# First layer's shift and scale by quarters of the features, with the first products behind each quarter

## Chip, cores and metric

The kernel runs on one core of a Trainium2 chip. The metric is the device time of one execution in microseconds (us). Three runs of the kernel before gave a median of 1486.53 us (1484.78 to 1489.08).

## What is computed

Two layers of a block over 1024 tokens x and 256 context tokens ctx with 1024 features, all in float32:

```
shift, scale, gate = split(silu(c) @ w_mod[l] + b_mod[l], 3)     # the same from c_ctx for ctx
h  = rms_norm(x, g_pre[l]) * (1 + scale) + shift                 # hc for ctx
y  = token_mixers(h @ w_in[l], hc @ w_in[l], ...)                # retention, spatial gating, short conv, gated delta
x  = x + gate * rms_norm(y @ w_out[l], g_post[l])                # ctx too, in layer 0
```

w_mod[l] has 1024 x 3072 elements, w_in[l] 1024 x 3856. So all of shift and scale (8.4 MB of w_mod) stands ahead of the first complete h of layer 0, and h ahead of every product with w_in. Feature j of h needs only columns j of shift and scale.

## The kernel before, in words

Tokens (x, then ctx) are cut into 10 tiles of 128 and into blocks of 512, 512 and 256; features are cut into 8 chunks of 128 (`KC`). h lies with features on partitions, as a high part h·h and a low part h·l (h minus its rounded high part); a weight is split in the same way into `whi` (ScalarE, line 479) and `wlo` (GpSimd, line 480). Each product is made of three matmuls: high by high, high by low, low by high. There are two kinds: token-major (`proj_tm`, PSUM tile `pt`, 272 columns with the gates' 16, lines 574 to 576; 24 matmuls a token tile) and feature-major (`projs`, PSUM tile `pj`, lines 540 to 542; 24 matmuls a block).

`first_h` is the first stage. It loads x of tiles 0 to 3, squares and sums each row (line 389), scales it (line 393), and turns it on TensorE (line 398). `mod(0)` loads w_mod in 16 loads of 128 rows by 1024 columns (line 266), first all of the shift, then all of the scale; each step makes four matmuls (line 268) that sum over the feature chunks, so shift and scale are known only when the last load has been used. `end` copies the sums, turns them and adds bias and g_pre (lines 278 to 289). Then `block` makes h for a block: block 0 (lines 434, 435, 439) from x turned beforehand, blocks 1 and 2 after a turn (lines 437 to 439); every third chunk's low part is made by GpSimd. `block(b)` also asks for x of the next block; it is called when `proj_tm` reaches tiles 0, 4 and 8.

The first product is `spatial_v` (token-major, with the gates); after it `gates`, then the key projection of the gated delta mixer (`delta_pair(l, 1)`, columns from 12 x 256, two strips of 128 columns over three blocks), and later the other mixers, drawn as filler beside the delta stages (`fillers`, `beside`).

All loads are issued from SyncE's one queue. `inorder` keeps the loads of the first stage in the order in which they are written down; otherwise the framework's planner orders each engine's instructions from dependencies and durations that it assumes, and lays the buffers in memory. A buffer's number of copies is its pool's: G 10, F 7, `q` 8, `raw` 2, `whi` and `wlo` 4; the next use of a copy waits until the one before is done.

`retention_pair` works block by block: scores `rsc` on TensorE (line 853), the scores times a constant mask on VectorE (line 857, mask kept in `base`), q times decay into `rqd` (line 863), then products into `ro` (lines 874, 881). `make_h` makes h of layer 1 beside the output products of layer 0 (lines 443 to 471).

Of the kernel before, what the change touches and what calls it, by code (L numbers as in the profile page):

```python
# [12 lines left out]
ALU = mybir.AluOpType  # L13
# [17 lines left out]
START = 5  # L31
KEPT = 2400
# [62 lines left out]
class Block:  # L95


    def __init__(self, ctx, tc, a, dbg=None):
        self.tc, self.nc, self.a, self.dbg = tc, tc.nc, a, dbg
        pool = lambda n, b, **k: ctx.enter_context(tc.tile_pool(name=n, bufs=b, **k))  # L100
        self.hp = pool("hp", 1)
        self.wp = pool("wp", 2)
        self.gp = pool("gp", 10)
        self.fp = pool("fp", 7)
        self.mp = pool("mp", 2)
        self.pj = pool("pj", 2, space=PSUM)
        self.pg = pool("pg", 2, space=PSUM)
        self.pf = pool("pf", 2, space=PSUM)
        self.pc = pool("pc", 1, space=PSUM)
        self.dp = pool("dp", 1, space=DRAM)  # L110
        self.uid = 0
        self.flow = iter(())
        self.lead = 0.0
        self.later = []
        self.loaded = None
        self.Hs = None
        self.both = {}
        self.rot = None
        self.layer = 0
# [56 lines left out]
    def setup(self):  # L176
# [4 lines left out]
                     ((C_ID, C_MASK), (C_MASK, C_TRI))}  # L181
# [75 lines left out]
    def mod(self, l):  # L257

        nc, a = self.nc, self.a
        pm = []  # L260

        def one(kc, half):
            if not pm:
                pm.append(self.pc.tile([P, 1024], F32, tag="cc", name="mod0"))
            w = self.slot("wm")[:, :D]
            self.inorder(nc.sync.dma_start(w, a["w_mod"][l, kc * P:(kc + 1) * P, half * D:(half + 1) * D]))
            for g in range(4):
                self.modded = nc.tensor.matmul(pm[0][32 * g:32 * g + 32, 256 * half:256 * half + 256], lhsT=self.s2[:, kc, :],
                                               rhs=w[:, 256 * g:256 * g + 256], start=(kc == 0), stop=(kc == KC - 1))

        def rows(half):
            if not pm:
                pm.append(self.psf("mod"))
            return pm[0][:, 256 * half:256 * half + 256]

        def end(half):
            ms = self.small([P, 256], "ms", 1)
            nc.scalar.copy(ms, pm[0][:, 256 * half:256 * half + 256])
            pt = self.psf("modT")
            for j in range(2):  # L280
                nc.tensor.transpose(pt[:, 128 * j:128 * j + 128], ms[:, 128 * j:128 * j + 128], self.ident)
            v = pt[:, :256].rearrange("p (j g q) -> p g j q", j=2, q=32)
            bm = self.fv[:, self.FV[("bmod", l)]].rearrange("p (s g j) -> p s g j", s=2, g=4)[:, half]
            gp = self.fv[:, self.FV[("gpre", l)]].rearrange("p (g j) -> p g j", g=4)
            for r in range(2):
                x = self.AB[l][:, r, 1 - half].rearrange("p (g j) -> p g j", g=4)
                nc.vector.tensor_tensor(x, v[:, :, :, r], bm, ALU.add)
                if half:
                    nc.vector.scalar_tensor_tensor(x, x, 1.0, gp, ALU.add, ALU.mult)

        steps = []
        for half in range(2):
            if l:
                steps += self.mod_rows(l, half, lambda half=half: rows(half))
            else:
                steps += [lambda kc=kc, half=half: one(kc, half) for kc in range(KC)]
            steps.append(lambda half=half: end(half))
        return steps

    def mod_rows(self, l, part, out):  # L300
# [11 lines left out]
        def step(j):  # L312
# [3 lines left out]
            with self.tc.manual_schedule(engines={PE}):  # L316
                for kc in (2 * j, 2 * j + 1):
                    for g in range(4):
                        nc.tensor.matmul(ps[32 * g:32 * g + 32], lhsT=self.s2[:, kc, :], rhs=w[kc, g // 2][:, 256 * (g % 2):256 * (g % 2) + 256],
                                         start=(kc == 0), stop=(kc == KC - 1))  # L320

        return [lambda: load(0)] + [lambda j=j: step(j) for j in range(KC // 2)]

    def quarter(self, nm):
        self.uid += 1
        return self.mp.tile([P, 512], F32, tag=f"q{self.layer}", name=f"{nm}{self.uid}", bufs=8)
# [49 lines left out]
    def first_h(self):  # L376
# [23 lines left out]

        self.new_h(0)
# [3 lines left out]
        for i, step in enumerate(self.mod(0)):  # L405
            if i == KC:
                turn_rows()
            step()
            if i < KC:
                for x in loads[i::KC]:  # L410
                    x()
            if START <= i < START + KC:
                kc = i - START
                if kc % 2 == 0:
                    xT.append(self.slot("xT", "G")[:, :1024].rearrange("p (j n) -> p j n", j=2))
                nc.scalar.copy(xT[-1][:, kc % 2], turn(kc, 0, 512, self.modded))

        def block(b, t0, n):
            if b < 2:
                t1 = t0 + n  # L420
                load(range(t1 // P, (t1 + BLOCKS[True][b + 1][1]) // P))
# [5 lines left out]
            A, B = self.AB[0][:, t0 // TL, 0], self.AB[0][:, t0 // TL, 1]  # L427
            for kc in range(KC):
                if kc % 2 == 0:
                    hb = xT[kc // 2] if b == 0 else self.slot("hb")[:, :2 * n].rearrange("p (j n) -> p j n", j=2)  # L430
                hf = hb[:, kc % 2]
                hi, lo = (self.h(s, kc, t0, n) for s in range(2))
                if b == 0:
                    nc.scalar.activation(hi, hf, AF.Identity, bias=B[:, kc:kc + 1], scale=A[:, kc:kc + 1])
                    nc.vector.tensor_scalar(hf, hf, A[:, kc:kc + 1], B[:, kc:kc + 1], ALU.mult, ALU.add)
                else:
                    nc.scalar.activation(hf, turn(kc, t0, n), AF.Identity, bias=B[:, kc:kc + 1], scale=A[:, kc:kc + 1])
                    nc.vector.tensor_copy(hi, hf)
                (nc.gpsimd if kc % 3 == 2 else nc.vector).tensor_tensor(lo, hf, hi.bitcast(F32), ALU.subtract)

        self.ahead = [lambda b=b, t0=t0, n=n: block(b, t0, n) for b, (t0, n) in enumerate(BLOCKS[True])]

    def make_h(self, l, t, x, held):
# [10 lines left out]
        xn = self.small([P, D], "xn", 1)  # L454
        nc.vector.tensor_scalar(xn, x, rs, None, ALU.mult)
        A, B = self.AB[l][:, r, 0], self.AB[l][:, r, 1]
        for q in range(2):
            pt = self.psf("xT")
            for j in range(4):
                kc = 4 * q + j  # L460
                self.after(nc.tensor.transpose(pt[:, j * P:(j + 1) * P], xn[:, kc * P:(kc + 1) * P], self.ident), held)
            hf = xn[:, 512 * q:512 * q + 512]
# [67 lines left out]
    def projs(self, l, blocks, *pairs):  # L530
# [3 lines left out]
        for t0, n in blocks:  # L534
            if self.ahead:
                self.ahead.pop(0)()
            for (hi, lo), (_, evac) in zip(W, pairs):
                b = self.bank("pj")
                for kc in range(KC):
                    nc.tensor.matmul(b[:, :n], lhsT=hi[kc], rhs=self.h(0, kc, t0, n), start=(kc == 0), stop=False)  # L540
                    nc.tensor.matmul(b[:, :n], lhsT=hi[kc], rhs=self.h(1, kc, t0, n), start=False, stop=False)  # L541
                    self.recent = nc.tensor.matmul(b[:, :n], lhsT=lo[kc], rhs=self.h(0, kc, t0, n), start=False, stop=(kc == KC - 1))  # L542
                    if kc % 2 and kc < KC - 1:
                        yield 6 * n / 2400
# [5 lines left out]

    def proj_tm(self, l, c0, tiles, evac, gates=False):

        nc = self.nc
        c1 = 15 * 256
        n = 272 if gates else 256
        w = []
        for j in range(4):
            hi, lo = (self.wtile(t, 2, n) for t in ("whi", "wlo"))
            raw = self.raw([P, 2, n])
            k = slice(2 * j, 2 * j + 2)  # L560
            self.inorder(nc.sync.dma_start(raw[:, :, :256], self.wcols(l, c0, 256)[:, k]))
            if gates:
                self.inorder(nc.sync.dma_start(raw[:, :, 256:], self.wcols(l, c1, 16)[:, k]))
            self.halve(hi, lo, raw)
            w.append((hi, lo))
        for t in range(NT if gates else len(tiles)):
# [3 lines left out]
            b = self.bank("pt")[:, cols]  # L570
            for kc in range(KC):
                hi, lo = (x[:, kc % 2, cols] for x in w[kc // 2])
                ah, al = (self.h(s, kc, t * P, P) for s in range(2))
                nc.tensor.matmul(b, lhsT=ah, rhs=hi, start=(kc == 0), stop=False)  # L574
                nc.tensor.matmul(b, lhsT=ah, rhs=lo, start=False, stop=False)  # L575
                nc.tensor.matmul(b, lhsT=al, rhs=hi, start=False, stop=(kc == KC - 1))  # L576
                if kc == 3:
                    yield 1.28
# [199 lines left out]
    def retention_pair(self, l, ctx, rp):  # L778
# [65 lines left out]
        mask = cst(C_MASK + rp * 256, 256).rearrange("p (h i) -> p h i", h=2)  # L844
        for t0, m in blocks:
            tiles = range(t0 // P, (t0 + m) // P)
            sc = []
            pSs = [self.psf("rsc") for _ in range(2)]
            with self.tc.manual_schedule(engines={PE}):
# [10 lines left out]
            qd = self.slot("rqd")[:, :2 * m].rearrange("p (d i) -> p d i", d=2)  # L860
# [720 lines left out]
    def run(self, out, layers=2):  # L1581
        self.setup()
        self.first_h()
        for l in range(layers):
# [3 lines left out]
            self.cols, self.made = self.columns(l), {}  # L1588
# [46 lines left out]
```

## Time and profile before

| | |
|---|---|
| median of 3 runs | 1486.53 us |
| profiled execution | 1490.67 us, its span 1488.9 us |
| mean granted TensorE clock | 0.957 |
| TensorE (PE) busy | 1383.5 us, 93% of the span |
| VectorE (DVE) busy | 733.0 us, 49% |
| ScalarE (ACT) busy | 452.7 us, 30% |
| GpSimd (POOL) busy | 332.6 us, 22% |
| chain that ended last, by engine | PE 73%, DVE 9%, issue 6%, DMA 4%, ACT 3%, POOL 3% |

Times are us from the start of the span. PE is TensorE's matmuls and PEld its weight loads; SPq are the loads that SyncE issues. A row of the timeline gives start, duration, engine, line, operation, output and inputs, and in brackets how long the engine was idle before it and what ended that. The granted clock is a share of 2.4 GHz; 0.50 is 1.2 GHz. A DMA share is the mean busy share of the 16 DMA engines in a stretch.

### The profile page before, as it was taken

To read this page: it belongs to the slowest core of one execution; us is meant where nothing else is said; L and a number is where in the kernel's file an instruction comes from. 1 tells how busy PE (TensorE), PEld (TensorE's weight loads), DVE (VectorE), ACT (ScalarE), POOL (GpSimd) and SP (SyncE) were. 2 spreads that over 40 slices of the span, in tenths; PEclk is the share of its full clock that TensorE was granted. 3 is DMA by queue.
4 is the path that set the end of the run, shared out by engine and by line. 5 is a ranking of instruction groups with operands and counts; after the bars stand their busy time and mean duration, and the time that the engine had idled before them with its cause. 6 is when DMAs were issued, how large, how long until landed. Compare 5 with 4: busy or idle time off the path is not lost.

```text
span 1488.9 us, 36109 instructions
## 1 busy us (share of the span) xinstructions
PE 1383.5 (93%) x15800; PEld 1154.1 (78%) x15800; DVE 733.0 (49%) x1357; ACT 452.7 (30%) x930; POOL 332.6 (22%) x265
## 2 busy tenths in 40 slices
PE   5789899889999999999999997997899999999997
PEld 2588788756787877788999985886667867878997
DVE  1657587244334746133444366395453476633132
ACT  3636422211201222332455536312121112233221
POOL 0233321112201311132122135112232112123220
PEclk9799979899999999999999998998899999999999
DMA  8415564126432212184234243635143103225451
GB/s 269 158 36 136 110 160 114 60 69 218 137 104 65 88 43 79 29 259 139 91 125 134 75 86 95 141 101 126 53 136 101 36 16 124 76 79 186 139 178 57
DMA packets 228392, 164.93 MB, mean 111 GB/s; under 512 B 112038, under 2 KB 195978, under 8 KB 228234
## 3 DMA queue, kind: packets, MB, share of 16 engines
q1 hardware_dynamic: 228234, 162.62, 37.5%
q8 instruction: 124, 2.03, 0.5%
q14 instruction: 34, 0.28, 0.1%
HBM read 122.34 MB, written 40.24 MB: 109 GB/s over the span
## 4 chain that ended last, share of the span: by engine, by line
PE 73%; DVE 9%; issue 6%; DMA 4%; ACT 3%; POOL 3%; SPq 0%; DVEq 0%; POOLq 0%; ACTq 0%
PE pj L540 13%; PE pj L541 12%; PE pj L542 12%; PE po L1526 4%; PE po L1528 4%; PE po L1527 4%; PE pt L574 3%; PE pt L576 2%; PE pt L575 2%; DMA wm<-in_w_mod 2%; PE gu L1316 1%; POOL wlo L480 1%; DVE lt L1158 1%; PE ro L874 1%; PE iq L1190 1%
## 5 line engine op out<-in xcount | busy, mean ns | idle before, releaser
L480 POOL TENSOR_TENSOR wlo<-raw,whi 128x512 fp32r<-128x512 f32 (+3 forms) x160 | 223.1, 1409 | 872.3 <-ACT whi L479 750.2
L540 PE MATMUL pj<-h0h,whi 128*128 128x512 f32 (+1 forms) x544 | 214.6, 394 | 11.3 <-ACT whi L479 10.6
L542 PE MATMUL pj<-h0h,wlo 128*128 128x512 f32 (+1 forms) x544 | 208.1, 382 | 4.7 <-POOL wlo L480 4.7
L540 PE MATMUL pj<-h1h,whi 128*128 128x512 f32 (+1 forms) x544 | 208.6, 383 | 0.0
L541 PE MATMUL pj<-h0l,whi 128*128 128x512 f32 (+1 forms) x544 | 207.7, 382 | 0.0
L541 PE MATMUL pj<-h1l,whi 128*128 128x512 f32 (+1 forms) x544 | 203.4, 374 | 0.0
L542 PE MATMUL pj<-h1h,wlo 128*128 128x512 f32 (+1 forms) x544 | 202.9, 373 | 0.5 <-POOL wlo L480 0.5
L1526 PE MATMUL po<-wo,whi 128*128 128x256 f32 x576 | 163.5, 284 | 1.8 <-DVE hf L1552 1.5
L1528 PE MATMUL po<-wo,wlo 128*128 128x256 f32 x576 | 162.2, 282 | 0.8 <-POOL wlo L480 0.8
L1527 PE MATMUL po<-wo,whi 128*128 128x256 f32 x576 | 162.0, 282 | 0.0
L540 PEld LDWEIGHTS pj<-h0h,whi 128*128 128x128 f32 x544 | 106.4, 196 | 32.3 <-ACT whi L479 10.9
L542 PEld LDWEIGHTS pj<-h0h,wlo 128*128 128x128 f32 x544 | 106.1, 195 | 24.9 <-POOL wlo L480 6.0
L541 PEld LDWEIGHTS pj<-h0l,whi 128*128 128x128 f32 x544 | 106.3, 195 | 19.6 <-issue 3.2
L542 PEld LDWEIGHTS pj<-h1h,wlo 128*128 128x128 f32 x544 | 103.2, 190 | 20.3 <-POOL wlo L480 1.4
L540 PEld LDWEIGHTS pj<-h1h,whi 128*128 128x128 f32 x544 | 103.5, 190 | 19.1 <-issue 0.4
L541 PEld LDWEIGHTS pj<-h1l,whi 128*128 128x128 f32 x544 | 103.6, 191 | 18.1 <-issue 1.9
L479 ACT CAST whi<-raw 128x512 fp32r<-128x512 f32 (+3 forms) x160 | 92.2, 607 | 65.9 <-DMA raw<-yd 28.2
L1526 PEld LDWEIGHTS po<-wo,whi 128*128 128x128 f32 x576 | 108.9, 189 | 3.6 <-DVE hf L1552 3.5
L1528 PEld LDWEIGHTS po<-wo,wlo 128*128 128x128 f32 x576 | 108.7, 189 | 1.0 <-POOL wlo L480 1.0
L1527 PEld LDWEIGHTS po<-wo,whi 128*128 128x128 f32 x576 | 108.8, 189 | 0.0
L1552 DVE TENSOR_TENSOR hf<-po,G 128x512 f32<-128x512 f32 x36 | 24.8, 689 | 123.1 <-ACT hg L1550 110.2
L1550 ACT ACTIVATE hg<-po 128x512 f32<-128x512 f32 x36 | 21.5, 598 | 113.6 <-PE po L1528 113.6
(287 smaller groups left out, 2323.5 us busy)
## 6 DMA issues: line engine op xcount, KB each, us to landing
raw<-in_w_in SPq DMA_DIRECT2D x120, 256.0 KB
wm<-in_w_mod SPq DMA_DIRECT2D x64, 256.0 KB
x<-in_x SPq DMA_DIRECT2D x16, 512.0 KB
wm<-in_w_mod SPq DMA_DIRECT2D x16, 512.0 KB
raw<-yd SPq DMA_DIRECT2D x32, 256.0 KB
gR<-gc SPq DMA_DIRECT2D x32, 160.0 KB
nd<-gR SPq DMA_DIRECT2D x16, 320.0 KB
gR<-Ad SPq DMA_DIRECT2D x18, 256.0 KB
```

The lines of the kernel that those rows point to most:

```text
L479: self.nc.scalar.copy(hi, raw)
L480: (engine or self.nc.gpsimd).tensor_tensor(lo, raw, hi.bitcast(F32), ALU.subtract)
L540: nc.tensor.matmul(b[:, :n], lhsT=hi[kc], rhs=self.h(0, kc, t0, n), start=(kc == 0), stop=False)
L541: nc.tensor.matmul(b[:, :n], lhsT=hi[kc], rhs=self.h(1, kc, t0, n), start=False, stop=False)
L542: self.recent = nc.tensor.matmul(b[:, :n], lhsT=lo[kc], rhs=self.h(0, kc, t0, n), start=False, stop=(kc == KC - 1))
L574: nc.tensor.matmul(b, lhsT=ah, rhs=hi, start=(kc == 0), stop=False)
L575: nc.tensor.matmul(b, lhsT=ah, rhs=lo, start=False, stop=False)
L576: nc.tensor.matmul(b, lhsT=al, rhs=hi, start=False, stop=(kc == KC - 1))
L1526: nc.tensor.matmul(b, lhsT=yh[kc], rhs=self.W[0, kc, j], start=kc == 0 and jj == 0, stop=False, skip_group_check=True)
L1527: nc.tensor.matmul(b, lhsT=yh[kc], rhs=self.W[1, kc, j], start=False, stop=False, skip_group_check=True)
L1528: held = nc.tensor.matmul(b, lhsT=yl[kc], rhs=self.W[0, kc, j], start=False, stop=kc == KC - 1 and jj == 1, skip_group_check=True)
L1552: nc.vector.tensor_tensor(tmp, pos[i][hf], g[:, 512 * hf:512 * hf + 512], ALU.mult)
```

## The change

`mod(0)` is replaced by four steps over quarters of the features. `scales(g)` loads the columns of quarter g of shift and of scale, all 1024 rows in one load each (two loads of 1 MB with rows of 1 KB, four buffers in all, so two quarters), makes 32 matmuls of 128 columns, and the two chunks' shift and scale. After each quarter come a quarter of the weights of `spatial_v` (and with every second quarter half of those of the first key strip), h of block 0 for the two chunks, and these chunks' products: of `spatial_v` for tiles 0 to 3, kept open in four PSUM banks (`begun`), and of the first key strip for block 0, kept open in half of the tile that also takes the shift and scale. x of tiles 4 to 7 is loaded right behind the fourth quarter.

The retention mask is no longer kept: each block loads its 128 KB into the tail of its `rqd` slot. `make_h` scales x in two halves that come from the ring `q`, and layer 1's `end` copies into a used quarter.

The core of the diff:

```diff
-START = 5
-KEPT = 2400
+KEPT = 1888
...
-                     ((C_ID, C_MASK), (C_MASK, C_TRI))}
+                     ((C_ID, C_MASK), (C_QD, C_TRI))}
...
-            ms = self.small([P, 256], "ms", 1)
+            ms = self.spare[:, :256]
...
+        def scales(g):
+
+            ws = []
+            for s in range(2):
+                self.uid += 1
+                ws.append(self.fp.tile([P, KC, 256], F32, tag="wq", name=f"wq{self.uid}", bufs=4))
+                self.inorder(nc.sync.dma_start(ws[s], a["w_mod"][0, :, s * D + 256 * g:s * D + 256 * g + 256].rearrange("(k p) n -> p k n", p=P)))
+            o = pm[:, P * g:P * g + P]
+            for kc in range(KC):
+                for j in range(4):
+                    nc.tensor.matmul(o[32 * j:32 * j + 32], lhsT=self.s2[:, kc, :], rhs=ws[j // 2][:, kc, P * (j % 2):P * (j % 2) + P],
+                                     start=(kc == 0), stop=(kc == KC - 1))
+            ms = self.quarter("ms")[:, :P]
+            nc.scalar.copy(ms, o)
+            pt = self.psf("modT")[:, :P]
+            nc.tensor.transpose(pt, ms, self.ident)
...
         self.new_h(0)
         load(range(4))
         xT = []
         loads, turn_rows = self.features()
...
+        for x in loads:
+            x()
+        turn_rows()
+        for kc in range(KC):
...
+            nc.scalar.copy(xT[-1][:, kc % 2], turn(kc, 0, 512))
+        pm = self.pc.tile([P, 1024], F32, tag="cc", name="mod0")
+
+        k0 = 12 * 256
+        wk = [self.slot("wk", "G", F32R)[:, :D].rearrange("p (k n) -> p k n", k=KC) for _ in range(2)]
+        self.made[k0] = tuple([w[:, kc] for kc in range(KC)] for w in wk)
+        self.begun = {t: self.bank("pt") if t < 2 else self.ps("pt") for t in range(4)}
+        self.begun[k0, 0] = pm[:, 512:]
+        self.tmw = []
+        for g in range(4):
+            scales(g)
+            self.tmw.append(self.tm_piece(0, 5 * 256, g, 272))
+            if g % 2 == 0:
+                k = slice(2 * g, 2 * g + 4)
+                self.halves(wk[0][:, k], wk[1][:, k], self.raw([P, 4, P]), self.wcols(0, k0, P)[:, k])
+            for kc in (2 * g, 2 * g + 1):
+                modulate(0, kc, 0, 512)
+            for t in range(4):
+                self.tm_products(self.begun[t][:, :272], t, (2 * g, 2 * g + 1), self.tmw, slice(0, 272))
+            self.fm_products(self.begun[k0, 0], 0, 512, (2 * g, 2 * g + 1), self.made[k0])
+        load(range(4, 8))
...
-        self.ahead = [lambda b=b, t0=t0, n=n: block(b, t0, n) for b, (t0, n) in enumerate(BLOCKS[True])]
+        self.ahead = [lambda: None] + [lambda b=b: block(b, *BLOCKS[True][b]) for b in (1, 2)]
...
-        xn = self.small([P, D], "xn", 1)
-        nc.vector.tensor_scalar(xn, x, rs, None, ALU.mult)
+        xs = [self.quarter("xn") for _ in range(2)]
+        for q, xn in enumerate(xs):
+            nc.vector.tensor_scalar(xn, x[:, 512 * q:512 * q + 512], rs, None, ALU.mult)
...
+                b = self.begun.pop((c0, t0), None)
+                if b is None:
...
-        mask = cst(C_MASK + rp * 256, 256).rearrange("p (h i) -> p h i", h=2)
...
+            qd = self.slot("rqd")
+            mask = qd[:, TL:TL + 256]
+            nc.sync.dma_start(mask, a["cst"][:, C_MASK + rp * 256:C_MASK + rp * 256 + 256])
+            mask = mask.rearrange("p (h i) -> p h i", h=2)
```

`modulate` is the body of `block` before; `tm_piece`, `tm_products` and `fm_products` are the bodies of `proj_tm`'s and `projs`'s loops, which now call them and skip what `begun` holds.

## Rows read from the trace of the kernel before

**Rows 1.** The page: busy us, share of the span and instructions of each engine.
```profile
PE 1383.5 (93%) x15800; PEld 1154.1 (78%) x15800; DVE 733.0 (49%) x1357; ACT 452.7 (30%) x930; POOL 332.6 (22%) x265
```

**Rows 2.** Busy time by stretches: us, each engine's busy time, PEclk, DMA share, GB/s.
```profile
0.00:45.00 45.00, 21.75 (x166) 8.46 (x166) 4.45 (x14) 14.97 (x25) 1.18 (x6) 0.90 0.76 249
45.00:80.00 35.00, 24.66 (x143) 21.62 (x144) 26.85 (x50) 27.63 (x42) 14.97 (x8) 0.79 0.46 149
80.00:142.00 62.00, 62.00 (x365) 54.81 (x364) 39.10 (x86) 28.32 (x58) 17.73 (x26) 0.97 0.34 76
142.00:154.00 12.00, 5.77 (x95) 4.80 (x94) 10.83 (x14) 11.32 (x17) 5.40 (x4) 0.90 0.33 101
```

**Rows 3.** The timeline of the first 50 us.
```profile
1.20 0.42 SPq L386 DMA_DIRECT2D x<-in_x  x1
...
5.13 1.06 ACT L389 ACTIVATE junk<-x 128x1024 f32<-128x1024 f32 x1 [3.11 <-DMA x<-in_x]
...
41.99 1.08 PE L268 MATMUL mod<-wm,base 128*32 128x256 f32 x8 [2.93 <-DMA wm<-in_w_mod]
...
45.57 1.52 ACT L434 ACTIVATE h0h<-xT,base 128x512 fp32r<-128x512 f32 x2 [1.46 <-DVE base L289]
...
46.44 0.59 PE L574 MATMUL pt<-whi,h0h 128*128 128x272 f32 x1 [2.13 <-ACT h0h L434]
...
49.38 9.48 SPq L386 DMA_DIRECT2D x<-in_x  x4
```

**Rows 4.** TensorE's matmuls in two stretches: us, busy (x), PEclk, DMA share, GB/s.
```profile
47.00:59.80 12.80, 10.55 (x47) 0.64 0.54 166
59.80:65.80 6.00, 6.00 (x51) 1.00 0.97 348
```

**Rows 5.** SyncE's waits up to 60 us: us in total, times, longest.
```profile
SPq L266 <- PE mod L268: 13.0, 13, 1.5
SPq L386 <- POOL wlo L480: 9.5, 2, 7.7
```

**Rows 6.** The timeline from 60 to 80 us: block 1's x and its h.
```profile
62.23 1.06 ACT L389 ACTIVATE junk<-x 128x1024 f32<-128x1024 f32 x1 [0.53 <-DMA x<-in_x]
...
73.71 5.72 POOL L439 TENSOR_TENSOR h0l<-hb,h0h 128x512 fp32r<-128x512 f32 x1 [15.20 <-DVE h0h L438]
...
79.39 1.27 POOL L439 TENSOR_TENSOR h1l<-hb,h1h 128x512 fp32r<-128x512 f32 x1
```

**Rows 7.** Stretches with loads of nearly one kind: the last two numbers count.
```profile
2.00:12.00 10.00, 0.25 (x1) 0.18 (x1) 0.00 (x0) 6.33 (x13) 0.00 (x0) 1.00 0.97 327
...
809.50:811.50 2.00, 2.00 (x19) 2.00 (x19) 0.11 (x1) 0.15 (x1) 2.00 (x2) 1.00 0.93 268
...
2.00:42.00 40.00, 20.00 (x158) 7.99 (x159) 3.43 (x8) 12.79 (x23) 0.00 (x0) 0.92 0.85 278
```

**Rows 8.** The chain that ended last: start, us, one key product of 512 columns.
```profile
105.24 0.23 PE pj L542
```

**Rows 9.** Who waited for line 857, the mask product: us in total, times.
```profile
  PEld ro L874: 1.8, 5
```

**Rows 10.** VectorE's timeline in the retention: layer 0, then layer 1.
```profile
540.52 1.28 DVE L863 TENSOR_TENSOR rqd<-rq,base 128x512 f32<-128x512 f32 x2
546.80 1.29 DVE L857 TENSOR_TENSOR hf<-rsc,base 128x512 f32<-128x512 f32 x2 [5.00 <-PE rsc L853]
...
1260.23 1.29 DVE L863 TENSOR_TENSOR rqd<-rq,base 128x512 f32<-128x512 f32 x2
...
1264.37 1.28 DVE L857 TENSOR_TENSOR hf<-rsc,base 128x512 f32<-128x512 f32 x2
```

**Rows 11.** The page's group of output products; the last numbers are idle before, releaser.
```profile
L1526 PE MATMUL po<-wo,whi 128*128 128x256 f32 x576 | 163.5, 284 | 1.8 <-DVE hf L1552 1.5
```

**Rows 12.** SyncE's timeline beside the retention of layer 0.
```profile
525.06 0.92 SPq L475 DMA_DIRECT2D raw<-in_w_in  x2
550.83 0.82 SPq L764 DMA_DIRECT2D rot<-in_rot  x2
```

More of the change, by code (lines that the diff above doesn't have):

```diff
@@ L116, in __init__ @@
         self.Hs = None
-        self.both = {}
+        self.both, self.made, self.begun, self.tmw = {}, {}, {}, None
         self.rot = None
@@ L260, in mod @@
         pm = []
[L262 to L269, printed above, removed]
         def rows(half):
@@ L292, in mod @@
         for half in range(2):
[L293 to L296, printed above, removed]
+            steps += self.mod_rows(l, half, lambda half=half: rows(half))
             steps.append(lambda half=half: end(half))
@@ L320, in step @@
                                          start=(kc == 0), stop=(kc == KC - 1))
+            self.spare = w[2 * j, 0]
         return [lambda: load(0)] + [lambda j=j: step(j) for j in range(KC // 2)]
@@ L325, in quarter @@
         self.uid += 1
-        return self.mp.tile([P, 512], F32, tag=f"q{self.layer}", name=f"{nm}{self.uid}", bufs=8)
+        return self.mp.tile([P, 544], F32, tag=f"q{self.layer}", name=f"{nm}{self.uid}", bufs=8)[:, :512]
     def gate(self, l):
@@ L399, in turn, with modulate @@
             return pt[:, :n]
+        hb = []
+        def modulate(b, kc, t0, n):
+            A, B = self.AB[0][:, t0 // TL, 0], self.AB[0][:, t0 // TL, 1]
+            if b and kc % 2 == 0:
+                hb.append(self.slot("hb")[:, :2 * n].rearrange("p (j n) -> p j n", j=2))
+            hf = (hb[-1] if b else xT[kc // 2])[:, kc % 2]
+            hi, lo = (self.h(s, kc, t0, n) for s in range(2))
+            if b == 0:
+                nc.scalar.activation(hi, hf, AF.Identity, bias=B[:, kc:kc + 1], scale=A[:, kc:kc + 1])
+                nc.vector.tensor_scalar(hf, hf, A[:, kc:kc + 1], B[:, kc:kc + 1], ALU.mult, ALU.add)
+            else:
+                nc.scalar.activation(hf, turn(kc, t0, n), AF.Identity, bias=B[:, kc:kc + 1], scale=A[:, kc:kc + 1])
+                nc.vector.tensor_copy(hi, hf)
+            (nc.gpsimd if kc % 3 == 2 else nc.vector).tensor_tensor(lo, hf, hi.bitcast(F32), ALU.subtract)
+        def scales(g):
[13 more added lines that the diff above has]
+            nc.tensor.transpose(pt, ms, self.ident)
+            v = pt.rearrange("p (s i q) -> p s i q", s=2, i=2)
+            f = lambda key, o: self.fv[:, self.FV[(key, 0)].start + o + 2 * g:self.FV[(key, 0)].start + o + 2 * g + 2]
+            for r in range(2):
+                for s in range(2):
+                    x = self.AB[0][:, r, 1 - s, 2 * g:2 * g + 2]
+                    nc.vector.tensor_tensor(x, v[:, s, :, r], f("bmod", KC * s), ALU.add)
+                    if s:
+                        nc.vector.scalar_tensor_tensor(x, x, 1.0, f("gpre", 0), ALU.add, ALU.mult)
         self.new_h(0)
@@ L404, in first_h @@
         loads, turn_rows = self.features()
[L405 to L416, printed above, removed]
+        for x in loads:
+            x()
+        turn_rows()
+        for kc in range(KC):
+            if kc % 2 == 0:
+                xT.append(self.slot("xT", "G")[:, :1024].rearrange("p (j n) -> p j n", j=2))
+            nc.scalar.copy(xT[-1][:, kc % 2], turn(kc, 0, 512))
[18 more added lines that the diff above has]
+        load(range(4, 8))
         def block(b, t0, n):
-            if b < 2:
-                t1 = t0 + n
-                load(range(t1 // P, (t1 + BLOCKS[True][b + 1][1]) // P))
+            if b == 1:
+                load(range(8, NT))
             else:
@@ L426, in block @@
                 self.loaded = None
-            A, B = self.AB[0][:, t0 // TL, 0], self.AB[0][:, t0 // TL, 1]
             for kc in range(KC):
[L429 to L439, printed above, removed]
-        self.ahead = [lambda b=b, t0=t0, n=n: block(b, t0, n) for b, (t0, n) in enumerate(BLOCKS[True])]
+                modulate(b, kc, t0, n)
+        self.ahead = [lambda: None] + [lambda b=b: block(b, *BLOCKS[True][b]) for b in (1, 2)]
     def make_h(self, l, t, x, held):
@@ L458, in make_h @@
             pt = self.psf("xT")
+            hf = xs[q]
             for j in range(4):
-                kc = 4 * q + j
-                self.after(nc.tensor.transpose(pt[:, j * P:(j + 1) * P], xn[:, kc * P:(kc + 1) * P], self.ident), held)
-            hf = xn[:, 512 * q:512 * q + 512]
+                self.after(nc.tensor.transpose(pt[:, j * P:(j + 1) * P], hf[:, j * P:(j + 1) * P], self.ident), held)
             for j in range(4):
@@ L536, in projs @@
                 self.ahead.pop(0)()
[L537 to L544, printed above, removed]
+            for w, (c0, evac) in zip(W, pairs):
+                b = self.begun.pop((c0, t0), None)
+                if b is None:
+                    b = self.bank("pj")
+                    for kc in range(0, KC, 2):
+                        self.fm_products(b, t0, n, (kc, kc + 1), w)
+                        if kc < KC - 2:
+                            yield 6 * n / 2400
                 for _ in range(2 if len(self.later) > KC else 1):
@@ L569, in proj_tm @@
             cols = slice(0, n) if t in tiles else slice(256, n)
[L570 to L578, printed above, removed]
+            b = self.begun.pop(t, None)
+            if b is None:
+                b = self.bank("pt")
+                for k in range(0, KC, 4):
+                    self.tm_products(b[:, cols], t, range(k, k + 4), w, cols)
+                    if k == 0:
+                        yield 1.28
+            b = b[:, cols]
             if t in tiles:
@@ L859, in retention_pair @@
                 sc.append(x)
-            qd = self.slot("rqd")[:, :2 * m].rearrange("p (d i) -> p d i", d=2)
+            qd = qd[:, :2 * m].rearrange("p (d i) -> p d i", d=2)
             for d in range(2):
@@ L1587, in run @@
             self.qkv, self.gz = [None] * 3, None
-            self.cols, self.made = self.columns(l), {}
+            self.cols = self.columns(l)
             self.flow = self.spatial_v(l, ctx)
```

36 lines of the change are left out of this document (25 added, 11 removed).

## The prediction, made before the result was known

> **What bounds the kernel now.** I read the page first, then the busy time by stretches. TensorE is busy for 93% of the span [rows 1], so a change of the first stage pays only where TensorE stands still or runs at the low clock. The stretches show where: up to 45 us it is busy 21.75 us, from 45 to 80 us 24.66 of 35 us at a mean granted clock of 0.79, and from 80 to 142 us all 62.00 us [rows 2]. After 142 us come 12 us in which VectorE and ScalarE are over 90% busy and TensorE 48%.
>
> The timeline of the first 80 us gives the order. The last products of the shift and scale wait for w_mod until 41.99 us; the first h starts at 45.57 us, the first product of h at 46.44 us [rows 3]. Products then come in pieces until 59.8 us (47 in 12.8 us, clock 0.64), and tiles 2 and 3 follow at full clock until 65.8 us (51 in 6.00 us) [rows 4]. Tokens 512 to 1023 hold up what comes next: their loads are issued from 49.38 us and stand 9.5 us behind GpSimd's low halves [rows 3, 5]; the last is there at 62.23 us, and the last h of block 1 is made by GpSimd at 79.39 us, after one subtraction that took 5.72 us [rows 6]. From there TensorE doesn't rest for 62 us. So two things count: when x of the second block has landed (A), and how much of the work after 80 us is already done by then (B).
>
> **The change part by part.** I work on the profiled execution: span 1488.9 us, 1490.67 us in all. That is 4.1 us over the median of 1486.53 us, and the gain in us is taken from the median.
>
> *Loads up to x of block 1.* Before, 16 loads of 512 KB in rows of 4 KB brought w_mod, and SyncE stood 13.0 us in 13 waits for TensorE's use of earlier buffers [rows 5]; over 2 to 42 us the DMA share was 0.85 [rows 7]. After, eight loads of 1 MB in rows of 1 KB bring it, two quarters in flight, so SyncE waits less often; but four w_in pieces (256 KB in rows of 1 KB, and 16 KB of gates) and two of 256 KB in rows of 512 B now stand in the same queue, three and two of them ahead of the last quarter. Rates by windows that hold nearly one kind: 4 KB rows 327 GB/s at a share of 0.97, 1 KB rows (w_in, at 809.5 us) 268 at 0.93 [rows 7], so 0.28 MB a us when the queue is full. From about 10 us, when x of block 0 has come (2.1 MB at 0.327, behind the 3.9 us of the first [rows 3]): small rows 0.5 us, w_mod 8.39 MB at 0.28 = 30.0 us, the pieces 1.11 MB = 4.0 us and 0.5 for the gates' 64-byte rows, the two others 0.52 MB = 1.9 us, x of block 1 2.1 MB at 0.33 = 6.4 us: 53.3 us if the queue never runs dry. Quarter 2 waits for the products of quarter 0 and quarter 3 for those of quarter 1, behind the transposes on TensorE; I add 2 us: x has landed at 55 us, against 62.23. At the share of 0.85 throughout, it would be about 60 us; with 1 KB rows as fast as 4 KB rows 49 us. A = 7 us, bounds 2 and 13.
>
> The Trainium skill (DMA: Bandwidth & Descriptors, Specifications) puts the shortest transfer at line rate at 512 B, so that rows of 1 KB would cost nothing, w_mod 25.7 us instead of 30.0; the trace disagrees (268 GB/s against 327 [rows 7]), and the sum goes by the trace. What that would make of the time is the third rival.
>
> What follows x is as before: squares, root, scaling, 32 transposes, h with the same 5.72 us on GpSimd. From landing to the last h took 18.4 us (62.23 to 80.7) [rows 6]; block 0's chain of the last quarter (about 48 to 57 us) lies ahead of it. So A carries through.
>
> *First products in the shade of the loads.* Each quarter gives 24 products of 272 columns and 6 of 512. At full clock 24 x 0.118 [rows 4] + 6 x 0.233 [rows 8] = 4.2 us, at the low clock twice that, some 8.4 us. A quarter's loads take some 9 us, so at worst TensorE ends level with them. The 32 products of the shift and scale have the columns of before. After the last quarter has landed (some 47.5 us) come copy, transposition, sums, h, and the last 30 products, until about 57 us: all hidden by the wait for x of block 1. What is gained is the first block of the key projection, 24 products of 512 columns, 24 x 0.233 = 5.6 us, which before stood in the stretch without rest [rows 2, 8]. That these 5.6 us go depends on the 12 us after 142 us, bounded by VectorE and ScalarE [rows 2]; VectorE has 22.9 us of slack in the 62 us ahead of it, so I count them whole. B = 5.6 us, bounds 0 and 5.6.
>
> *Mask reloaded.* The retention mask is no longer kept; each of 10 blocks loads 128 KB of it into the tail of its slot, ahead of the multiplication at line 857. That wait is new: behind it on VectorE stand the q-decay products (line 863), and TensorE's `ro`, which already waits 1.8 us in all for line 857 [rows 9]. The slot of the next block is free early in layer 0 (q-decay of block 1 at 540.52, its mask product only at 546.80); in layer 1 q-decay starts at 1260.23, its mask product at 1264.37 [rows 10]. From issue to use the first x, 512 KB, took 3.9 us (1.20 to 5.13) [rows 3]. So 4 to 6 us of cover meet a load of under 4 us: 0 in most blocks. Also the 20 multiplications are the same. Bounds: 0 and 6 reused slots x 3.9 = 23 us. I take 1 us, near the covered side, since every gap seen is at least as long as the load.
>
> *The rest.* make_h scales in two halves and takes both from the ring of quarters: TensorE stands 1.8 us in all before line 1526, the output products beside which make_h runs [rows 11], so nothing of it is on the path; 0, with bounds of 1.8 us either way (that rest gone, or doubled). Shift and scale of layer 1 copy into a used quarter instead of a tile of their own: 0, beside the same products. The constants' load is smaller by 256 KB and off the path. Buffers lie elsewhere and the order of instructions is planned anew for the whole kernel, at 0; the nearest row is TensorE's rest of 6.2 us in the 12 us after 142 us [rows 2], and half of one such stretch, 3 us, is allowed either way.
>
> Sum: -7 - 5.6 + 1 = -11.6 us: 1479.1 us against the profiled 1490.67, 1475 us against the median.
>
> **Rivals.**
> 1. *The loads come no sooner.* The releases of quarter buffers stand behind TensorE's 8.4 us of slow products, each quarter then starts late, and x lands at 60 us or after. For it: TensorE had a mean clock of 0.64 from 47 to 59.8 us, between its levels of 1.2 and 2.4 GHz, when it was fed in pieces [rows 4], and it will be fed in pieces. Against: quarter 2 is released by the 32 short products of quarter 0 alone. Then A = 1 and the time is 1486.5 - 1 - 5.6 + 1 = 1481. The Trainium skill (TensorE: Matmul & The Clock Gate, HAM oscillation) warns of just this loop, bursts of products between DMA waits, at the low clock; the trace of 47 to 59.8 us agrees (0.64).
> 2. *The end of the stretch is not TensorE's.* The keys' 5.6 us vanish in the 12 us bounded by VectorE and ScalarE. For it: both are over 90% busy there [rows 2]. Against: the slack ahead. Time: 1486.5 - 7 + 1 = 1480.5.
> 3. *More than forecast.* Rows of 1 KB flow as fast as rows of 4 KB once 1 MB is asked for at a time: x lands at 49 us, A = 13, time 1469.
> 4. *Slower: the masks.* SyncE is one queue and stood from 525.98 to 550.83 us before the rotation tables, waiting for slots [rows 12]. If mask loads go out only when `ro` is due, `ro` and all products behind it stand for the whole load: 6 reused slots x 3.9 = 23 us, 1486.5 - 12.6 + 23 = 1497. It decides from 2.1 us a slot. Against: the mask is asked for ahead of the tables in the program, and slots were free in layer 0.
>
> **How the numbers follow.** Forecast 0.55, rivals 0.14, 0.10, 0.13, 0.08. What a measurement of this kernel tells from no change is about 0.3%, 4.5 us. Faster by more: the forecast but for 0.03, rival 3, half of rival 1 and two thirds of rival 2: 0.79. Slower: rival 4 and 0.02 for a plan gone wrong: 0.10. Within: 0.11. The forecast's own range is 1468 to 1482; for 8 in 10 it reaches into rivals 1 and 3 and the replanning: 1463 to 1487.
>
> **What would show it.** In the profile after: the first h near 22 to 26 us, not 45.57; the last w_mod landed near 47 us, x of block 1 near 55; squares of those x from 50 us; the 24 products of keys' block 0 before 60 us and tile 4 starting near 62; TensorE without rest from about 73 us, and keys done about 12 us earlier than 142 us. The mask loads would be seen landing before line 857 starts, with waits of `ro` as short as 0.4 us. The forecast is wrong if x of block 1 lands after 60 us, if TensorE's rest after the keys grows by what was won, or if waits for the mask load show at line 857.

## The result, and the profile after

The kernel after takes 1472.46 us (median of 9 runs, 1470.13 to 1480.97), the kernel before beside it 1486.53 (9 runs, 1483.97 to 1489.08): ratio 0.9916, 95% interval 0.9895 to 0.9937. The forecast was 1475. The profiled execution of after has a span of 1475.4 us against 1488.9, and 1477.17 us in all, so it too lies over its median, by 4.7 us.

The page's busy times, as [rows 1]:

```profile
PE 1378.5 (93%) x15928; PEld 1156.9 (78%) x15928; DVE 741.5 (50%) x1385; ACT 450.3 (31%) x930; POOL 325.9 (22%) x265
```

Busy time by stretches, as [rows 2, 7]: us, busy time of PE, PEld, DVE, ACT and POOL, granted clock, DMA share, GB/s:

```profile
0.00:45.00 45.00, 26.91 (x276) 22.98 (x280) 11.80 (x28) 19.52 (x33) 8.73 (x11) 0.89 0.91 285
45.00:80.00 35.00, 26.03 (x230) 21.42 (x219) 20.86 (x53) 24.24 (x38) 5.38 (x4) 0.95 0.42 134
80.00:142.00 62.00, 60.70 (x423) 53.35 (x423) 46.38 (x96) 32.93 (x68) 19.13 (x25) 1.00 0.32 78
142.00:154.00 12.00, 12.00 (x135) 9.55 (x133) 11.93 (x16) 8.02 (x10) 7.05 (x5) 1.00 0.00 1
...
10.00:44.00 34.00, 25.66 (x239) 21.81 (x243) 11.44 (x25) 13.36 (x23) 8.36 (x6) 0.85 1.01 311
44.00:46.00 2.00, 1.59 (x61) 1.32 (x49) 0.00 (x0) 0.27 (x1) 0.00 (x0) 1.00 0.02 8
44.00:54.00 10.00, 7.70 (x123) 6.41 (x115) 2.35 (x9) 3.37 (x6) 2.60 (x2) 1.00 0.27 75
```

TensorE does more before 80 us (52.9 us against 46.4) and mostly at the high clock; the stretch behind the keys, where it stood for half the time, is full. The last three rows: to 44 us the DMA queues are full at 311 GB/s, then they fall silent (share 0.02), while most of x of block 1 has yet to be asked for.

The timeline of after where [rows 3, 6] stood:

```profile
24.27 1.52 ACT L398 ACTIVATE h0h<-xT,base 128x512 fp32r<-128x512 f32 x2 [1.84 <-DVE base L426]
...
40.28 12.61 SPq L374 DMA_DIRECT2D x<-in_x  x4
...
43.62 1.95 PE L415 MATMUL mod<-wq,base 128*32 128x128 f32 x64
...
53.12 1.95 PE L415 MATMUL mod<-wq,base 128*32 128x128 f32 x64
...
58.96 1.06 ACT L377 ACTIVATE junk<-x 128x1024 f32<-128x1024 f32 x1
...
63.72 1.42 DVE L381 TENSOR_SCALAR x<-x,ssum 128x1024 f32<-128x1024 f32 x2
...
73.32 1.39 POOL L403 TENSOR_TENSOR h0l<-hb,h0h 128x512 fp32r<-128x512 f32 x1 [21.27 <-DVE h0h L402]
73.50 1.50 DVE L402 CAST h1h<-hb 128x512 fp32r<-128x512 f32 x1
74.77 0.39 PE L601 MATMUL pt<-whi,h0l 128*128 128x272 f32 x1 [0.60 <-POOL h0l L403]
...
78.22 1.28 DVE L403 TENSOR_TENSOR h1l<-hb,h1h 128x512 fp32r<-128x512 f32 x2
```

Block 0's h starts at 24.27 us, as forecast. The last quarter's products start at 53.12 us though their weights are there by 44; the four loads of x are issued over 12.61 us; the last h of block 1 ends at 79.50 us, against 80.66 before. One thing is quite different: GpSimd's subtraction takes 1.39 us, not 5.72, and TensorE waits 0.60 us for it.

SyncE's waits up to 60 us, as [rows 5]:

```profile
SPq L374 <- PE modT L420: 5.6, 1, 5.6
SPq L374 <- POOL wlo L512: 5.2, 1, 5.2
SPq L588 <- DVE h0l L403: 5.0, 1, 5.0
SPq L411 <- PE mod L415: 4.6, 2, 3.6
```

And who was waited for ahead of `ro`, as [rows 9]; line 909 is the mask product:

```profile
  DVE hf L909: 1.8, 5
```

To see where time is won, start times of the same VectorE and ScalarE instructions were subtracted, after minus before, and the median taken by stretches of the run (us; the others are the experiments below; all against before's profiled execution, which lies 4.1 us over its median):

```
stretch   after    e3     e5     e7     e8    e12
 85-95     -5.4   -7.6   -7.6  -14.4  -16.2   -9.2
135-145    -9.8   -8.4  -12.0  -17.6  -15.6   -7.1
270-290   -18.3  -14.8  -18.2  -26.1  -16.9   -9.8
400-430   -14.5  -13.6  -19.0  -24.7  -18.9  -11.8
1400-end  -13.3  -15.8  -16.8  -27.1  -17.5  -11.7
```

So in this profile after is 5.4 us ahead when the token-major tiles end, 4.4 more with the keys, 8.5 more by 270 us, and 3.8 are given back by 400 us.

### The profile page after: what moved, and what is told of

It is laid out like the page before. It is cut to its first block, busy times and chain, and to the rows that moved or that the text cites. A ratio compares the mean times of both kernels' runs of the same rounds, so it can differ in the third digit from the quotient of the medians.

```text
span 1475.4 us, 36425 instructions
## 1 busy us (share of the span) xinstructions
PE 1378.5 (93%) x15928; PEld 1156.9 (78%) x15928; DVE 741.5 (50%) x1385; ACT 450.3 (31%) x930; POOL 325.9 (22%) x265
## 4 chain that ended last, share of the span: by engine, by line
PE 72%; DVE 11%; issue 7%; ACT 4%; DMA 3%; POOL 2%; SPq 0%; DVEq 0%; POOLq 0%; ACTq 0%
PE pj L607 13%; PE pj L608 12%; PE pj L609 12%; PE po L1578 4%; PE po L1580 4%; PE po L1579 4%; PE pt L599 3%; PE pt L601 2%; PE pt L600 2%; PE gu L1368 2%; DVE lt L1210 1%; PE ro L926 1%; POOL wlo L512 1%; PE ip L1253 1%; PE iq L1242 1%
## 5 line engine op out<-in xcount | busy, mean ns | idle before, releaser
L512 POOL TENSOR_TENSOR wlo<-raw,whi 128x512 fp32r<-128x512 f32 (+3 forms) x158 | 217.0, 1388 | 845.9 <-ACT whi L511 719.3
L607 PE MATMUL pj<-h0h,whi 128*128 128x512 f32 (+1 forms) x532 | 211.3, 397 | 8.8 <-ACT whi L511 6.0
L609 PE MATMUL pj<-h0h,wlo 128*128 128x512 f32 (+1 forms) x532 | 203.5, 383 | 3.1 <-POOL wlo L512 3.1
L608 PE MATMUL pj<-h0l,whi 128*128 128x512 f32 (+1 forms) x532 | 203.8, 383 | 0.0
L607 PE MATMUL pj<-h1h,whi 128*128 128x512 f32 (+1 forms) x532 | 203.4, 382 | 0.0
L608 PE MATMUL pj<-h1l,whi 128*128 128x512 f32 (+1 forms) x532 | 199.2, 374 | 0.0
L609 PE MATMUL pj<-h1h,wlo 128*128 128x512 f32 (+1 forms) x532 | 198.2, 373 | 0.1
L607 PEld LDWEIGHTS pj<-h1h,whi 128*128 128x128 f32 x532 | 101.1, 190 | 18.4 <-issue 0.4
```

The source lines that it names most:

```text
L512: (engine or self.nc.gpsimd).tensor_tensor(lo, raw, hi.bitcast(F32), ALU.subtract)
```

## The experiments

Of the time to 95 us, the traces said: the last h comes 1.2 us sooner, GpSimd's shorter subtraction gives 4. Differences below are of medians. Each median was taken beside the kernel before (1486.39 to 1486.77 us), and the ratios to it have intervals of 2 to 3 us either way, so two runs less than some 3 us apart can't be told from each other. Theory: GpSimd's subtraction and the keys' products make the gain; rival: the forecast's, an earlier x.

**e1, e2: products left where they were.** e1 drops the begun key products, e2 all begun products:

```diff
-        self.begun[k0, 0] = pm[:, 512:]
-            self.fm_products(self.begun[k0, 0], 0, 512, (2 * g, 2 * g + 1), self.made[k0])
# e2 also:
-        self.begun = {t: self.bank("pt") if t < 2 else self.ps("pt") for t in range(4)}
-            for t in range(4):
-                self.tm_products(self.begun[t][:, :272], t, (2 * g, 2 * g + 1), self.tmw, slice(0, 272))
```

> The kernel after, but the 24 key products of block 0 are not begun in the first stage; they stand where they stood before. Theory (the keys' block is paid for its TensorE time): 24 x 0.233 = 5.6 us more than after, 1478 us. Rival (the stretch after the keys is VectorE's and ScalarE's and eats the gain): no more than 1 us over after, 1472 to 1473.5 us, with TensorE idle again only behind the keys. A shift between 2 and 9 us that first appears after 146 us would say that the plan of later stages, not the products themselves, carries part of it.

> The kernel after, with shift, scale and h of block 0 by quarters as they are, but no product begun: tiles 0 to 3 (96 products of 0.118 us, 11.3 us) and the keys' block 0 (5.6 us) come behind the last quarter. Theory (what ends the first stage is block 1's h at 79.5 us, so 11.3 us of products still fit between 57 and 79 us): as without the keys alone, 1478 us, within 1.5 us of it. Rival (the products in the shade of the loads are themselves the gain): 1478 + 11.3 = 1489 us, no gain left.

e1 took 1487.29 us (ratio to before 0.9999, 0.9983 to 1.0015): the whole gain gone, far over either theory. e2 took 1478.50 (0.9927, 0.9910 to 0.9945), as its theory said, although it leaves out more. In e1 GpSimd's long subtraction is back, and TensorE's wait with it:

```profile
70.75 5.72 POOL L403 TENSOR_TENSOR h0l<-hb,h0h 128x512 fp32r<-128x512 f32 x1 [20.80 <-DVE h0h L402]
...
76.53 0.59 PE L599 MATMUL pt<-whi,h0l 128*128 128x272 f32 x1 [4.19 <-POOL h0l L403]
```

In e2 it took 1.66 us. So e1 mixes two things, and the token products begun early are worth nothing by themselves: e2, which has none, is no slower than e6 below, which has them.

**e3, e4: parts put into the kernel before.** e3 takes GpSimd out of block 1; e4 takes over the side edits alone.

```diff
# e3
-                (nc.gpsimd if kc % 3 == 2 else nc.vector).tensor_tensor(lo, ...)
+                (nc.gpsimd if kc % 3 == 2 and b != 1 else nc.vector).tensor_tensor(lo, ...)
```

> The kernel before, with the two low halves of block 1 that GpSimd made now made by VectorE. Theory (of the 5.4 us that after is ahead at 95 us, 4.5 come from GpSimd's subtraction that took 5.72 us before and 1.39 after, for which TensorE stood 4.55 us at 79.5 us, and not from an earlier x): 3 to 4.5 us less than before, 1482 to 1483.5 us; the wait at 79.5 us gone or under 1 us. Rival (the forecast's: the landing of x of block 1 sets this stage): same as before within 1 us, 1486.5 us.

> The kernel before, with only the side edits: mask reloaded for each block, h of layer 1 scaled in two halves, a used quarter for layer 1's sums, and the buffers' new sizes. Theory: masks cost about 1 us and the rest nothing, 1486 to 1489 us. Rival 1 (the new plan that comes with the edits brings the gains seen from 146 to 235 us): 3 to 8 us less, 1478 to 1483 us, and those shifts show at the same places. Rival 2 (reloading is dear and hidden in the sum): 1492 us or more.

e3: 1480.77 us (0.9946, 0.9925 to 0.9967), 5.7 us less, more than its theory said; the wait is gone and the clock stays up. (Its profile is 2.3 us ahead already when x of block 1 is first asked for, at 47.04 us, where the edit has not acted yet.) The same stretch of e3 and of before:

```profile
60.00:80.00 20.00, 18.60 (x146) 17.59 (x145) 15.43 (x41) 17.04 (x29) 0.00 (x0) 1.00 0.33 110
```

```profile
60.00:80.00 20.00, 13.35 (x96) 11.71 (x95) 13.34 (x34) 16.65 (x26) 6.29 (x2) 0.91 0.44 150
```

The rival that x's landing alone sets the stage falls. e4: 1482.56 us (0.9968, 0.9954 to 0.9982), 4.0 less: neither what the theory nor quite what rival 1 said, for the shift is not made from 146 to 235 us but stands at 10.0 us at 60 to 80 us already, by the subtraction of the table. e12 below explains it.

**e5, e6: the same with GpSimd out of the way.** e3's edit in after (e5), and e1's with it (e6).

> The kernel after, with the two low halves of block 1 that GpSimd makes given to VectorE. In after GpSimd's two took 1.39 us each and two of VectorE's casts took 1.50 instead of 0.42 us beside them, so the exchange is about even. Theory: same as after within 2 us, 1470.5 to 1474.5 us, with no wait of TensorE for GpSimd at 74 to 79 us. Rival (after is slowed by GpSimd in most runs and the profile showed a lucky one): 3 us or more below after, under 1469.5 us.

> As e5, and the keys' block 0 not begun in the first stage (the edit of e1). Theory (of the 15 us by which e1 stood behind after, some 4 were GpSimd's 5.72 us subtraction that came back there, and 5.6 are the 24 key products): 5 to 7 us over e5, about 1478 us. Rival (the key block moves the plan of the later stages, and that is most of the 15 us): 10 us or more over e5, with shifts that first show after 146 us.

e5: 1475.06 us (0.9915, 0.9896 to 0.9933); 0.6 us over its theory's range, by the interval the same as after. e6: 1480.34 (0.9958, 0.9944 to 0.9973), 5.3 us more, as its theory said: the keys' price as forecast. e3 and e5 now differ by the change alone, without GpSimd: the last h of block 1 ends at 77.66 and 77.34 us, so an earlier x brings 0.3 us there, or 2.6 if e3's early start is taken off. Then e1 - e6 = 7.0 us is the price of GpSimd's long subtraction, and e4 - e8 = 6.4 says it again: three pairs, 5.7 to 7.0 us, where the profile showed 5.72 us; no gain where it showed 1.39 (after and e5).

**e8: no quarters at all.** The side edits and e3's edit together, w_mod by rows.

> The kernel before with the side edits (e4) and block 1's low halves on VectorE (e3): w_mod is still loaded by rows, no product is begun early. Theory (e3 and e4 gain at separate places, 5.7 and 4.0 us): 1476 to 1479 us, so that the quarters themselves are worth only what is left to after, about the keys' 5.6 us. Rival (the two gains are the same one, a sooner block 1): 1480 to 1483 us.

1476.19 us (0.9921, 0.9905 to 0.9938): e3 and e4 add up. This kernel has none of the change's reordering, and is within 4 us of after. Against e6, which has the quarters but not the keys, it is 4.2 us faster, and the intervals don't meet: the quarters, with x of block 1 asked for behind them, cost. The last h of block 1 ends at 68.99 us in e8 and at 74.99 in e6.

**e12: the mask alone**, put into the kernel before.

```diff
-KEPT = 2400
+KEPT = 1888
-                     ((C_ID, C_MASK), (C_MASK, C_TRI))}
+                     ((C_ID, C_MASK), (C_QD, C_TRI))}
# and the mask's load into the tail of rqd, as in the change
```

> The kernel before with one of the side edits alone: the retention mask is not kept but loaded for each block. Theory (the 2 KB a partition that it frees let five loads of w_mod stand at a time instead of three, and that is the whole of e4's gain): the sixth load, not the fourth, is the first to wait for a product; last products of shift and scale at 32 to 34 us instead of 43, x of block 1 asked for at 36 to 39 us; time as e4, 1481 to 1485 us, GpSimd's 5.72 us subtraction still there. Rival (the gain of e4 is from make_h's halves or the ring's new size, and the mask costs): 1486 us or more.

1478.07 us (0.9949, 0.9933 to 0.9965): 8.4 us less than before, more than the theory said, though x of block 1 is asked for only at 41.01 us. SyncE's loads of w_mod in e12, its last products of shift and scale, and GpSimd:

```profile
6.47 0.49 SPq L266 DMA_DIRECT2D wm<-in_w_mod  x1
9.48 0.33 SPq L266 DMA_DIRECT2D wm<-in_w_mod  x1
11.96 0.33 SPq L266 DMA_DIRECT2D wm<-in_w_mod  x1
13.30 0.33 SPq L266 DMA_DIRECT2D wm<-in_w_mod  x1
...
33.06 0.64 PE L268 MATMUL mod<-wm,base 128*32 128x256 f32 x8 [0.64 <-DMA wm<-in_w_mod]
...
63.73 5.73 POOL L439 TENSOR_TENSOR h0l<-hb,h0h 128x512 fp32r<-128x512 f32 x1 [14.56 <-DVE h0h L438]
```

and one stretch of e12:

```profile
16.00:28.00 12.00, 11.41 (x103) 4.95 (x99) 1.04 (x4) 4.36 (x8) 0.00 (x0) 1.00 1.01 386
```

The products by which each load had been issued show how many loads stood at a time: in before the fourth load went out at 13.49 us, behind the first load's 8 products, and at each later one three stood open; in e12 the fourth and fifth went out at 9.48 and 11.96 us with no product done, and five to six stand. The queue then runs full (386 GB/s from 16 to 28 us; before 288), the last products start at 33.06 us instead of 41.99 [rows 3]. So the room of the mask, 2 KB a partition, let two or three more loads of w_mod stand. How the planner made buffers of 5 KB a partition (`SLOT`) out of it is not shown. Of the three side edits, this one is enough. e4, which has it too, gained less (4.0), but its interval and e12's overlap. By the subtraction of the table both are about 9 us ahead at 85 to 95 us (9.0 and 9.2); only behind 290 us do their profiles part, to 4.5 and 11.7 us at the end. Why is open.

**e9: rows of 4 KB** in after's eight loads.

```diff
-    ...dma_start(ws[s], a["w_mod"][0, :, s * D + 256 * g:s * D + 256 * g + 256].rearrange("(k p) n -> p k n", p=P))
+    ...dma_start(ws[s].rearrange("p (j k) n -> p j (k n)", j=2),
+                 a["w_mod"][0, 256 * g:256 * g + 256, s * D:s * D + D].rearrange("(j p) n -> p j n", p=P))
```

> As e5, but each of the eight loads of w_mod brings 256 whole rows by 1024 columns, rows of 4 KB as in before, into the same buffers at the same places; shift and scale are then computed from the wrong elements, all else is as it is. Theory (1 KB rows flow at 268 GB/s and 4 KB rows at 327, so the eight loads lose 4.3 us): last products of shift and scale some 4 us earlier, x of block 1 4 us earlier, 2 to 5 us below e5, 1470 to 1473 us. Rival (SyncE's waits for buffers, not the rows, set the loads): last quarter within 1.5 us of after's 53.1 us, time within 1.5 us of e5.

1472.76 us (0.9911, 0.9893 to 0.9930). The time alone doesn't decide: it is 2.3 us below e5, in the theory's range, but the same as e5 by the interval. The last quarter decides: its loads are issued at 33.80 us (after: 33.24), its products start at 53.68 us, and x comes no sooner. The first 45 us of e9, then 16 to 28 us of e9 and of after:

```profile
0.00:45.00 45.00, 26.40 (x256) 22.45 (x260) 12.81 (x28) 19.51 (x33) 9.02 (x11) 0.89 0.81 285
...
16.00:28.00 12.00, 9.28 (x103) 8.40 (x102) 4.30 (x12) 7.67 (x14) 3.62 (x3) 0.94 1.05 391
```

```profile
16.00:28.00 12.00, 9.27 (x104) 8.57 (x103) 3.95 (x10) 7.14 (x13) 2.56 (x2) 0.92 1.12 340
```

To 45 us the same 285 GB/s as in after, at a share of 0.81 instead of 0.91. Short rows do cost queue time (with the queue full, 340 GB/s in after, 391 in e9), but that time was free. The Trainium skill (DMA: Bandwidth & Descriptors, Specifications) puts the shortest transfer at line rate at 512 B, so that rows of both lengths should run alike; these two figures disagree. For the kernel's time it is no matter. The rival holds in its mechanism: releases, not rows, set the pace of the quarters.

**e7, e10, e11: x of block 1 sooner.** e7 asks for it ahead of the last quarter; e10 also makes six chunks of block 1 before the last quarter's, e11 asks ahead of the third quarter.

```diff
         for g in range(4):
+            if g == 3:                 # e11: 2
+                load(range(4, 8))
+                # e10, e11: modulate(1, kc, 512, 512) for the chunks whose shift and scale are there
             scales(g)
...
-        load(range(4, 8))
```

> As e5, but x of block 1 is asked for ahead of the last quarter of w_mod instead of behind it: x should land near 50 us instead of 59, the last quarter some 6 us later. Theory (from x's landing to the last h VectorE works without rest, so the stage ends that much sooner when VectorE can begin sooner): last h of block 1 at 72 to 75 instead of 79.5 us, 4 to 7 us below e5, 1465 to 1469 us. Rival (the last quarter is as late as x was, so the end of the stage stays): within 1.5 us of e5 or slower.

> As e7, and block 1's chunks 0 to 5 are turned and made while the last quarter is still loading, in PSUM banks that the open products don't hold (in e7 most of block 1's turns stood behind tiles 0 to 3 until 63 us). Theory (only the last two chunks are then left when the last quarter comes): last h of block 1 at 61 to 64 instead of 70.4 us, 5 to 8 us below e7, 1456 to 1460 us. Rival (ScalarE and VectorE, or TensorE, become the bound between 52 and 62 us): within 2 us of e7.

> As e10, with x of block 1 ahead of the third quarter already, so that its chunks follow quarters 2 and 3 too. Theory (VectorE's and ScalarE's work on block 1 spreads over 40 to 60 us): last h of block 1 1 to 3 us before e10's, time 0 to 3 us below e10. Rival (quarters 2 and 3 start later, and block 0's own chain ends later): 1 to 4 us above e10.

e7: 1464.32 us (0.9860, 0.9840 to 0.9880), the fastest kernel here, 10.7 us below e5, more than its theory said. Its last square of that x, last quarter and last h of block 1:

```profile
47.28 1.06 ACT L377 ACTIVATE junk<-x 128x1024 f32<-128x1024 f32 x1
...
52.50 1.94 PE L415 MATMUL mod<-wq,base 128*32 128x128 f32 x60 [0.40 <-DMA wq<-in_w_mod]
...
69.10 1.29 DVE L403 TENSOR_TENSOR h1l<-hb,h1h 128x512 fp32r<-128x512 f32 x2
```

x is squared 11.7 us sooner than in after, the last quarter is used no later (the queue had been silent), and the last h ends at 70.39, 9.1 us sooner than in after. e10 (1470.69; 0.9891, 0.9869 to 0.9912) and e11 (1469.66; 0.9889, 0.9871 to 0.9906) are slower than e7 by medians, with intervals that still touch e7's; the 5 to 8 us below e7 of e10's theory are ruled out. e11 did against e10 what its theory said (1.0 us less; its last h, at 70.44 us, comes even sooner than said), but it gained nothing on e7: its last h comes no sooner, and its last quarter is used from 57.74 us. In e10 the last quarter's products (64 records) were put between block 1's turns, which wait for ScalarE:

```profile
54.21 0.41 PE L415 MATMUL mod<-wq,base 128*32 128x128 f32 x2
...
60.27 1.29 PE L415 MATMUL mod<-wq,base 128*32 128x128 f32 x38
62.47 0.33 PE L420 MATMUL modT<-base,ms 128*128 128x128 f32 x1 [0.91 <-ACT ms L418]
```

1.95 us of products took 7.4, and the last h ended at 76.36 us. So neither number for e10 came, neither the theory's nor its rival's (within 2 us of e7); in kind it is the rival: work made ready early got in front of what was late.

## Why the prediction was right, and where it wasn't

The number was right (1475 forecast, 1472.46 measured), for one of its two reasons. That the other's failure doesn't show in it is luck: gains that the forecast had put at nothing stand in its place.

*B, the keys: right.* 5.6 us forecast; e6 minus e5 is 5.3, the table shows 4.4 between 95 and 135 us of after, and TensorE's rest behind the keys did not grow by what was won (6.2 us from 142 to 154 us before; now 0 there, and 2.5 from 154 to 166). Rival 2 falls. That the 12 us from 142 us are full now (12.00) is not the keys' doing: they are full in e1 too, where no keys are begun.

*A, x of block 1: the step failed*, in two places. The smaller is "I add 2 us" for waits. The loads ran faster than summed (340 GB/s from 16 to 28 us, where the sum had 280): all that was asked for was there by about 45 us, the last quarter forecast at 47.5. But then SyncE stood 5.6 and 5.2 us ahead of x, and by the landing records of the trace the last of x came at 57.0 us, not 55. Against 62.1 before, that is still 5.2 of the 7 us.

The larger is "all hidden by the wait for x of block 1" and "So A carries through". Block 0's last quarter ended at 62.0 us, not 57, so its work stood among x's, in the order of ScalarE:

```profile
55.17 0.27 ACT L418 COPY ms<-mod 128x128 f32<-128x128 f32 x1 [5.26 <-PE mod L415]
55.33 1.06 ACT L377 ACTIVATE junk<-x 128x1024 f32<-128x1024 f32 x1
...
56.38 1.51 ACT L398 ACTIVATE h1h<-xT,base 128x512 fp32r<-128x512 f32 x2
57.79 1.04 ACT L377 ACTIVATE junk<-x 128x1024 f32<-128x1024 f32 x1
...
60.13 1.28 ACT L705 ACT_TABLE_LOAD   x1
61.42 0.39 ACT L705 ACTIVATE sv<-pt 128x256 f32<-128x256 f32 x1
```

The copy of the last quarter's sums (line 418) and two chunks of block 0's h (line 398) stand ahead of the last two squares (line 377). ScalarE stood idle for 5.26 us ahead of that copy, though the second tile of x, squared behind it, had landed at 50.0 us. The last square of x starts at 58.96 us, 2.0 us after x landed, and waits for no load; in before it waited for one [rows 6]. In after, e5, e9 and e7 alike it starts 3.79 us behind the copy of a quarter's sums, in e7 the third quarter's. A table load and a GELU more (line 705) then lay between that square and the scaling (4.8 us, before 3.1). From landing to the last h it took 22.5 us, not 18.4, and the last h came 1.2 us sooner: A = 1.2, not 7.

Rival 1 had that size, though x landed before its 60 us, and a cause of the right kind: TensorE works in order, so the third quarter's products, weights long there, stood behind the 30 products of the second. From 33 to 44 us it was fed in pieces at a mean granted clock of 0.69, between its two levels (0.50 and 1.00):

```profile
33.00:44.00 11.00, 8.80 (x55) 6.90 (x51) 4.40 (x9) 2.84 (x5) 4.45 (x3) 0.69 0.92 286
```

e7 shows that A was there to be had, and e9 that the rows (rival 3) were not what kept it.

*"The same 5.72 us on GpSimd": wrong.* Taken over as a fixed duration, it was a wait. Its fall to 1.39 us gave 4 us of the 5.4 at 95 us; e3, e6 and e8 price it at 5.7 to 7.0. It made up for most of A. Nobody had planned that: e1 has the same loads and got the wait back.

*The mask: no wait, 0 for the forecast 1.* `ro` waited 1.8 us in 5 times for line 909, as for line 857 [rows 9]; rival 4 falls. What the step missed is the room: in the kernel before, the mask alone is worth 8.4 us. What that room is worth inside the change was not tested.

*The replanning, at 0 within 3 us: too narrow.* Between 145 and 290 us after wins 8.5 us more, and loses 3.8 by 400 us. All twelve others gained there too against before's profile, from 1.3 us (e8) to 9.7 (e10). Which orders of later work do it is not settled by these runs.

## What to carry to other kernels

A long duration in a trace may be a wait inside the instruction: compare it with the same instruction elsewhere before it goes into a sum as fixed. Where loads pace a stage, count how many stand at a time and ask what releases them, in order, on every queue they pass; rate times bytes comes second. An input that has landed is not yet used: look at what stands ahead of its first use on the engine that takes it. And a side edit that frees memory is an edit to every buffer ring: price it alone.

## What the runs showed of the hardware

GpSimd's subtraction of 128x512 elements took 1.27 to 1.66 us when it got in, and then a cast of VectorE beside it took 1.50 instead of 0.42 us; or 5.72 us, when VectorE had ten instructions behind one another (73.55 to 78.31 us in before) and GpSimd ended only 1.1 us after the last. The start and the end of that run:

```profile
73.55 0.68 DVE L439 TENSOR_TENSOR h0l<-hb,h0h 128x512 fp32r<-128x512 f32 x1
74.15 0.42 DVE L438 CAST h0h<-hb 128x512 fp32r<-128x512 f32 x1
...
77.03 1.28 DVE L439 TENSOR_TENSOR h1l<-hb,h1h 128x512 fp32r<-128x512 f32 x2
```

Four profiles showed the second (before, e1, e4, e12), two the first (after, e2), on the same data and shapes. The Trainium skill (SBUF — State Buffer, SBUF: two separate sides) describes one pair of ports that whichever of VectorE and GpSimd starts first holds for a whole instruction, while the other blocks; the 1.50 us cast agrees. That GpSimd may stay out over a run of ten instructions, the rows show beyond it. What decides who gets in is open: in before and in e2 GpSimd started at the same point of VectorE's run, 0.16 and 0.17 us into a subtraction.
